# Four gathered value rows per burst, at the highest priority, with seven gather tiles and six steps between U and V

## The chip, the core and the metric

The kernel runs on one core of a Trainium2 chip. A core has five engines with queues of their own, each worked through in order: TensorE (PE; its weight loads are shown as PEld), VectorE (DVE), ScalarE (ACT), GpSimd (POOL) and SyncE (SP). Here SP issues the plain transfers and POOL the gathers. The metric is the device time of one execution in microseconds (us). Before the change it is 3000.16 us, the median of three runs (2996.83 to 3005.19).

## The reference, cut to what matters

Two layers, each a token mixer and then an expert mixer; 512 tokens of width 1024:

```
x = x + sliding_window_attention(rmsnorm(x), ...)      # layer 0
x = x + peer_ffn(rmsnorm(x), ..., peer_u[0], peer_v[0])
x = x + short_gated_conv(rmsnorm(x), ...)              # layer 1
x = x + peer_ffn(rmsnorm(x), ..., peer_u[1], peer_v[1])

def peer_ffn(...):   # per token: 8 heads, 16 of 16384 experts each
    s = scores of the query against 2 x 128 sub keys;  idx, g = top 16 of the sums, softmax
    a = einsum('td,thkd->thk', x, U[idx])
    w = g * gelu(a)
    y = einsum('thk,thkd->td', w, V[idx])
```

So every token needs 128 rows of U and 128 rows of V, of 4 KB each, chosen by its own routing.

## The kernel before, in words

The 512 tokens are four tiles of 128 (0 to 3). The expert mixer treats them in two ways.

**Tiles 2 and 3: dense.** `dense` runs through all 16384 experts in 128 steps of 128. `ustep(i)` loads 512 KB of U, splits it in a high and a low part (ACT casts, DVE subtracts: `uh`, `ul`), multiplies (24 matmuls into `psA`) and takes the gelu into `dw`. `vstep(i)` multiplies `dw` by the gates `G` (POOL or DVE, L713), splits it (`wh`, `wl`), loads and splits 512 KB of V (`vh`, `vl`) and adds 12 matmuls to the four accumulators `y` (L731). U steps run `LAG` = 7 ahead. The gates come from `gen` (L734 on): 64 generations a layer, made in four chunks of 16, each with three DVE operations (`igr`, `oj`, `oi`) and 32 small matmuls into `psG`; a V step needs the whole chunk of its 32 steps. The first chunk stands in a prelude between the routing and the first V step.

**Tiles 0 and 1: gathered.** `gather(l, t)` treats one tile of one layer; the four calls run one after the other. First the U rows: 128 gathers of 128 rows (512 KB, POOL, L631), each followed by a multiply and row sum on DVE (L634, `ug`). Then the V rows: 128 gathers (L662), one for each token, and each token's 128 rows are multiplied by its weights on PE, in matmuls with 32 output columns in the array (L672, `acc`). Tokens come in pairs, so that the two halves of two tokens use the four column groups at once: four matmuls a pair. All gather tiles come from the pool `gat` with `GAT` = 6 buffers (in front of layer 1's dense stage two more).

**Who sets the order.** `merge` interleaves three streams (dense and what precedes it; gathers; a routing stream for tiles 0 and 1) by due times; `DSTEP` = 6.8 for a dense step and `rate()`, 2.4 or 2.5 beside a dense stage, for a gather. That gives each instruction its place and so its priority; `tc.high_priority(offset)` raises it by so many places. A scheduler then writes each engine's queue, taking by priority what it holds to be ready. The queue's order is fixed before the kernel runs. The V matmuls have `HPV` = 600 beside a dense stage and `HPF` = 3000 elsewhere, `gen` has 3000, the U rows' operations on DVE 0. A manual dependency lets the first row's matmuls of a pair wait for the second row's gather, so that a pair stands together.

The calls follow each other as U1, V1 (layer 0, tile 0), U2, V2 (layer 0, tile 1), U3, V3 (layer 1, tile 0), U4, V4 (layer 1, tile 1). In the trace U2, V2 and most of U3 lie beside layer 0's dense stage, V3 beside the convolution and routing of layer 1, U4 and V4 beside layer 1's dense stage.

Of the kernel before, what the change touches and what calls it, by code (L numbers as in the profile page):

```python
# [8 lines left out]
F32 = mybir.dt.float32  # L9
# [10 lines left out]
P = 128  # L20
# [9 lines left out]
NK = 128  # L30
# [3 lines left out]
GONE = -3.0e38  # L34
TG = 16
IC = 32
GAT = 6
RB = 4
HB = 2
LB = 2  # L40
DSTEP = 6.8
LAG = 7
SCB = 4
HPG = 3000
HPT = 0
# [15 lines left out]
VB0 = 1.0  # L61
WPU = 1
WPV = 0
HPV = 600
HPF = 3000
GX0 = 0
FS0 = 1.0
FS1 = 1.0
# [14 lines left out]
def trunk(ctx: ExitStack, tc: tile.TileContext, a: dict, out: bass.AP):  # L83
    nc = tc.nc
# [441 lines left out]
    def router(l, tiles, rpool, psum, xnT, res):  # L526
        gain = gain_of(a["norm_ffn"][l:l + 1, :])
        early = l == 0 and tiles == [0]
        groups = []
        rs = {}  # L530
        dt = [t for t in tiles if t >= 2]
        for t in sorted(tiles, reverse=True):
            if t >= 2:
                rs[t] = route_alloc()
                normT(t, gain, xnT[:, :, (t - 2) * P:(t - 1) * P], psum)
            else:
                h = b4.tile([P, D], F32, name="h", tag="b4")
                norm(t, gain, h)
                nc.sync.dma_start(xnd[t], h)
                hT = gp.tile([P, KC, P], F32, name="hTr", tag="hTr", bufs=1)  # L540
                to_hT(h, hT, psum)
                groups.append((hT, P, [t]))
                if t == 0:
                    rs[t] = route_alloc()
            yield 5.0
        if dt:
            nc.scalar.copy(xh, xnT)
            nc.vector.tensor_tensor(xl, xnT, xh, op=ALU.subtract)
            groups.insert(0, (xnT, 2 * P, dt))
        for h in range(PH):  # L550
            kk = s2.tile([P, 2, NK], F32, name="kk")
            nc.sync.dma_start(kk, a["keysT"][l][:, 2 * h:2 * h + 2, :])
            ws = [piece(a["wq"][l, 2 * h + p]) for p in range(2)]
            for hT, T, js in groups:
                qT = (s2 if T == P else rpool).tile([P, 2, T], F32, name=f"rqT{T}", bufs=2)
                for p in range(2):
                    ps = psum("psrq")
                    if R3[l] and T > P:
                        tg, nb = (("sc", "sc"), SCB) if l == 0 else (("wh", "wl"), WSB)
                        mm3(ps[:, :T], split(ws[p], rpool, tg, nb), (xh, xl), slice(0, T))  # L560
                    else:
                        for k in range(KC):
                            nc.tensor.matmul(ps[:, :T], ws[p][:, k, :], hT[:, k, :],
                                             start=(k == 0), stop=(k == KC - 1))
                    nc.scalar.copy(qT[:, p, :T], ps[:, :T])
                for jj, t in enumerate(js):
                    ps = psum("psrs")
                    for p in range(2):
                        nc.tensor.matmul(ps[:, p * P:(p + 1) * P], qT[:, p, jj * P:(jj + 1) * P],
                                         kk[:, p, :], start=True, stop=True)  # L570
                    sc = s2.tile([P, 2, NK], F32, name="rsc", bufs=3)
                    nc.scalar.copy(sc, ps[:, :2 * P].rearrange("p (m k) -> p m k", m=2))
                    if t == 1:
                        nc.sync.dma_start(scd[h], sc)
                    else:
                        route_head(rs[t], h, sc)
                    if early:
                        decode(rs[t], h, h + 1)
                        expert_idx(rs[t], h, h + 1)
                        if h == 0:  # L580
                            res.append(rs[t])
                        st[f"h0_0_{h}"] = 1
                    elif t >= 2 and h % DEC == DEC - 1:
                        decode(rs[t], h + 1 - DEC, h + 1)
                    yield 4.5 * (3.0 if l == 1 and tiles == [0] else 1.0)
        for t in sorted(rs):
            if t < 2 and not early:
                decode(rs[t], 0, PH)
                expert_idx(rs[t], 0, PH)
            route_end(rs[t], t, psum)  # L590
            if not early:
                res.append(rs[t])
            yield 5.0

    def late_router(l, psum, res):
        r = route_alloc()
        for h in range(PH):
            sc = s2.tile([P, 2, NK], F32, name="rsc", bufs=3)
            nc.sync.dma_start(sc, scd[h])
            route_head(r, h, sc)  # L600
            decode(r, h, h + 1)
            expert_idx(r, h, h + 1)
            if h == 0:
                res.append(r)
            st[f"h{l}_1_{h}"] = 1
            yield LP
        route_end(r, 1, psum)
# [12 lines left out]
    def gather(l, t, r):  # L620
# [5 lines left out]
        for s in range(P):  # L626
            if early and s % TK == 0:
                yield f"h{l}_{t}_{s // TK}"
            h, c = divmod(s, TK)
# [19 lines left out]
        for gr in range(2):  # L649
            acc = pv.tile([P, 512], F32, name="acc", tag="acc")  # L650
            for q in range(4):
                wd = gp.tile([P, 2, 8, 32], F32, name="wd", tag="wd", bufs=2)
                wdf = wd.rearrange("p j r c -> p j (r c)")
                nc.gpsimd.memset(wd, 0.0)
                nc.vector.tensor_copy(wdf[:, :, 8 * q:8 * q + 7 * 33 + 1:33],
                                      wT.rearrange("p (j r) -> p j r", j=4)[:, 2 * gr:2 * gr + 2, 8 * q:8 * q + 8])
                for r8 in range(8):
                    vgs = []
                    for j in range(2):
                        tt = 64 * gr + 32 * j + 8 * q + r8  # L660
                        vg = gtile("vg")
                        ld = nc.gpsimd.indirect_dma_start(  # L662
                            out=vg, out_offset=None, in_=a[f"v{l}"],
                            in_offset=bass.IndirectOffsetOnAxis(ap=idxT[:, tt:tt + 1], axis=0))
                        vgs.append(vg)
                        if j == 0:
                            yield rate()
                    with tc.high_priority(offset=HPF if st.get("front") else HPV):
                        for j in range(2):
                            for h in range(2):  # L670
                                c = 32 * (2 * j + h)
                                mm = nc.tensor.matmul(acc[c:c + 32, :], wd[:, j, r8, :],  # L672
                                                      vgs[j][:, h * 512:(h + 1) * 512],
                                                      start=(q == 0 and r8 == 0), stop=(q == 3 and r8 == 7))
                                if j == 0:
                                    tc.add_manual_dep(mm.ins, ld.ins.name, together, reason="both rows of a pair")
                    yield rate()
            for j in range(2):
                for h in range(2):
# [308 lines left out]
```

## Time and profile before

| | |
|---|---|
| median of three runs | 3000.16 us |
| the profiled execution | 2992.02 us, span 2990.3 us |
| PE, PEld busy | 88%, 70% of the span |
| DVE busy | 75% |
| ACT, POOL busy | 52%, 46% |
| mean transfer rate | 311 GB/s |
| largest single groups | L631 U gathers on POOL 668.3 us, L634 on DVE 622.8 us, L672 V matmuls on PE 318.1 us |

The busy shares are averages over stages with different limits. The page's second part shows it: in some of the 40 slices PE stands at 9, in others DVE. So the span is to be read by stage, and in each stage the engine is to be found that has no idle time.

### The profile page before, as it was taken

The page shows a single profiled execution, that of the slowest core. Times are in us where ns is not written, and L with a number is a line of the kernel's source. Part 1 is how long each engine was busy: PE and PEld are TensorE (multiplying, and loading weights), DVE is VectorE, ACT ScalarE, POOL GpSimd, SP SyncE. Part 2 cuts the span into 40 slices and gives each one's busy share as a digit, 9 for nine tenths or more (in the row PEclk, how much of TensorE's full clock was granted, in tenths as well). Part 3 has the DMA queues.
Part 4 walks back from the last instruction along what each step waited for, and adds up shares of the span by engine and source line. Part 5 has one row for each costly group of instructions (what it writes and reads, how often), then busy time and mean ns, then how long its engine had stood idle before and what let it go on. Part 6 is the DMA issues. An engine that isn't in the chain of part 4 may idle for free. (4 is left out here: it accounts for less than half of the span.)

```text
span 2990.3 us, 53463 instructions
## 1 busy us (share of the span) xinstructions
PE 2626.9 (88%) x19980; PEld 2083.9 (70%) x19980; DVE 2235.7 (75%) x5234; ACT 1559.1 (52%) x2384; POOL 1365.3 (46%) x1154
## 2 busy tenths in 40 slices
PE   5974699869999889999998689997888699999998
PEld 5762368636988767777787686773677577777897
DVE  2499849888998987446699774899899957446554
ACT  4224533685673458348444333358466449547543
POOL 0157733366344455534467424236566755554000
PEclk8986799989999999999999799997999899999999
DMA  5888988989999988998999867789999998998554
GB/s 199 283 315 306 341 293 276 329 308 382 365 353 389 323 318 290 345 328 291 363 408 396 310 220 279 249 319 318 363 349 360 345 359 297 333 317 302 192 189 157
DMA packets 263204, 931.38 MB, mean 311 GB/s; under 512 B 29984, under 2 KB 38560, under 8 KB 262944
## 3 DMA queue, kind: packets, MB, share of 16 engines
q0 software_dynamic: 147456, 536.94, 49.5%
q1 hardware_dynamic: 115488, 391.03, 36.3%
q8 instruction: 157, 2.57, 0.3%
q14 instruction: 103, 0.84, 0.1%
HBM read 916.31 MB, written 11.53 MB: 310 GB/s over the span
## 5 line engine op out<-in xcount | busy, mean ns | idle before, releaser
L631 POOL DMA_INDIRECT ug<-in_u_dram,idx x512 | 668.3, 1305 | 638.1 <-DVE act L634 312.5
L662 POOL DMA_INDIRECT vg<-in_v_dram,idxT x512 | 572.2, 1118 | 689.1 <-PE acc L672 571.7
L634 DVE CUSTOM_DVE_ANT_0 ug<-ug,xn 128x1024 f32<-128x1024 f32 x512 | 622.8, 1226 | 40.3 <-DMA ug<-in_u_dram,idx 39.3
L176 PE MATMUL psA<-xh,uh 128*128 128x256 f32 x2048 | 521.1, 292 | 46.0 <-ACT uh L696 19.0
L177 PE MATMUL psA<-xl,uh 128*128 128x256 f32 x2048 | 504.2, 284 | 0.0
L176 PEld LDWEIGHTS psA<-xh,uh 128*128 128x128 f32 x2048 | 391.1, 191 | 127.9 <-ACT wh L719 32.7
L697 DVE TENSOR_TENSOR ul<-du,uh 128x1024 fp32r<-128x1024 f32 x256 | 316.6, 1237 | 181.0 <-ACT uh L696 179.1
L697 DVE TENSOR_TENSOR vl<-dv,vh 128x1024 fp32r<-128x1024 f32 x256 | 316.2, 1235 | 145.2 <-ACT vh L696 121.8
L177 PEld LDWEIGHTS psA<-xl,uh 128*128 128x128 f32 x2048 | 392.0, 191 | 4.5 <-issue 0.5
L696 ACT CAST uh<-du 128x1024 fp32r<-128x1024 f32 x256 | 268.6, 1049 | 205.3 <-PE psA L177 172.6
L696 ACT CAST vh<-dv 128x1024 fp32r<-128x1024 f32 x256 | 268.5, 1050 | 162.7 <-PE y L731 139.7
L672 PE MATMUL acc<-vg,wd 128*32 128x512 f32 x2048 | 318.1, 635 | 31.4 <-DMA vg<-in_v_dram,idxT 30.9
L731 PE MATMUL y<-vh,wh 128*128 128x512 f32 x1024 | 290.2, 406 | 34.9 <-ACT vh L696 29.9
L179 PE MATMUL psA<-xh,ul 128*128 128x256 f32 x2048 | 288.7, 283 | 10.1 <-DVE ul L697 10.0
L731 PE MATMUL y<-vl,wh 128*128 128x512 f32 x1024 | 285.7, 401 | 12.8 <-DVE vl L697 12.8
L731 PE MATMUL y<-vh,wl 128*128 128x512 f32 x1024 | 285.5, 399 | 3.0 <-DVE wl L720 3.0
L179 PEld LDWEIGHTS psA<-xh,ul 128*128 128x128 f32 x2048 | 261.8, 189 | 21.8 <-DVE ul L697 16.6
L738 ACT COPY jr<-ijg 128x2048 f16<-128x2048 f16 x128 | 243.2, 1900 | 35.0 <-DVE oj L742 33.1
L731 PEld LDWEIGHTS y<-vh,wh 128*128 128x128 f32 x1024 | 179.4, 191 | 86.5 <-ACT vh L696 36.7
L731 PEld LDWEIGHTS y<-vl,wh 128*128 128x128 f32 x1024 | 190.1, 191 | 62.9 <-DVE vl L697 18.8
L731 PEld LDWEIGHTS y<-vh,wl 128*128 128x128 f32 x1024 | 194.8, 192 | 50.9 <-DVE wl L720 4.7
L742 DVE TENSOR_TENSOR oj<-jr,io 128x2048 f16<-128x2048 f16 x128 | 157.4, 1229 | 78.0 <-PE psG L751 66.7
(208 smaller groups left out, 4021.1 us busy)
## 6 DMA issues: line engine op xcount, KB each, us to landing
du<-in_uT_dram SPq DMA_DIRECT2D x256, 512.0 KB, 6.6
dv<-in_v_dram SPq DMA_DIRECT2D x256, 512.0 KB, 5.9
wpc<-in_wq_dram SPq DMA_DIRECT2D x64, 512.0 KB, 4.8
wpc<-in_w_in_dram SPq DMA_DIRECT2D x48, 512.0 KB, 5.9
wpo<-in_wo_dram SPq DMA_DIRECT2D x16, 512.0 KB, 7.5
ug<-in_u_dram,idx POOLq DMA_INDIRECT x512
vg<-in_v_dram,idxT POOLq DMA_INDIRECT x512
wpo<-in_w_out_dram SPq DMA_DIRECT2D x16, 512.0 KB, 5.2
```

The costliest lines, as they stand in the source:

```text
L176: nc.tensor.matmul(ps, w[0][:, k, :], x[0][:, k, ts], start=(k == 0), stop=False)
L177: nc.tensor.matmul(ps, w[0][:, k, :], x[1][:, k, ts], start=False, stop=False)
L179: nc.tensor.matmul(ps, w[1][:, k, :], x[0][:, k, ts], start=False, stop=(k == KC - 1))
L631: nc.gpsimd.indirect_dma_start(out=ug, out_offset=None, in_=a[f"u{l}"], in_offset=bass.IndirectOffsetOnAxis(ap=r["idx"][h][:, c:c + 1], ax ...
L634: nc.vector.tensor_tensor_reduce(out=ug, in0=ug, in1=xn, scale=1.0, scalar=0.0, op0=ALU.mult, op1=ALU.add, accum_out=act[:, s:s + 1])
L662: ld = nc.gpsimd.indirect_dma_start(out=vg, out_offset=None, in_=a[f"v{l}"], in_offset=bass.IndirectOffsetOnAxis(ap=idxT[:, tt:tt + 1], ax ...
L672: mm = nc.tensor.matmul(acc[c:c + 32, :], wd[:, j, r8, :], vgs[j][:, h * 512:(h + 1) * 512], start=(q == 0 and r8 == 0), stop=(q == 3 and ...
L696: nc.scalar.copy(hi, w)
L697: nc.vector.tensor_tensor(lo, w, hi, op=ALU.subtract)
L731: nc.tensor.matmul(ys[tt][h], x[:, tt * P:(tt + 1) * P], m[:, h * 512:(h + 1) * 512], start=first and k == 0, stop=last and k == len(terms ...
L738: nc.scalar.copy(jr, ijg[:, 0, t0:t0 + TG].unsqueeze(2).to_broadcast([P, TG, P]))
L742: nc.vector.tensor_tensor(oj, jr, io128.unsqueeze(1).to_broadcast([P, TG, P]), op=ALU.is_equal)
```

## The change

- A group of V rows is four tokens instead of two (eight matmuls instead of four), and each row's matmuls wait for all later gathers of the group.
- `HPV` and `HPF` become 5000.
- `GAT` is 7, `LAG` is 6 (with two `dw` buffers beyond it, as before), and the score tile `rsc` has two buffers instead of three.

```diff
--- before.py
+++ after.py
@@ -34,12 +34,12 @@
 GONE = -3.0e38
 TG = 16
 IC = 32
-GAT = 6
+GAT = 7
 RB = 4
+LB = 2
 HB = 2
-LB = 2
 DSTEP = 6.8
-LAG = 7
+LAG = 6
 SCB = 4
 HPG = 3000
 HPT = 0
@@ -61,8 +61,8 @@
 VB0 = 1.0
 WPU = 1
 WPV = 0
-HPV = 600
-HPF = 3000
+HPV = 5000
+HPF = 5000
 GX0 = 0
 FS0 = 1.0
 FS1 = 1.0
@@ -568,7 +568,7 @@
                     for p in range(2):
                         nc.tensor.matmul(ps[:, p * P:(p + 1) * P], qT[:, p, jj * P:(jj + 1) * P],
                                          kk[:, p, :], start=True, stop=True)
-                    sc = s2.tile([P, 2, NK], F32, name="rsc", bufs=3)
+                    sc = s2.tile([P, 2, NK], F32, name="rsc", bufs=2)
                     nc.scalar.copy(sc, ps[:, :2 * P].rearrange("p (m k) -> p m k", m=2))
                     if t == 1:
                         nc.sync.dma_start(scd[h], sc)
@@ -595,7 +595,7 @@
     def late_router(l, psum, res):
         r = route_alloc()
         for h in range(PH):
-            sc = s2.tile([P, 2, NK], F32, name="rsc", bufs=3)
+            sc = s2.tile([P, 2, NK], F32, name="rsc", bufs=2)
             nc.sync.dma_start(sc, scd[h])
             route_head(r, h, sc)
             decode(r, h, h + 1)
@@ -654,26 +654,28 @@
                 nc.gpsimd.memset(wd, 0.0)
                 nc.vector.tensor_copy(wdf[:, :, 8 * q:8 * q + 7 * 33 + 1:33],
                                       wT.rearrange("p (j r) -> p j r", j=4)[:, 2 * gr:2 * gr + 2, 8 * q:8 * q + 8])
-                for r8 in range(8):
-                    vgs = []
-                    for j in range(2):
-                        tt = 64 * gr + 32 * j + 8 * q + r8
+                for r8 in range(0, 8, 2):
+                    vgs, lds = [], []
+                    for n in range(4):
+                        tt = 64 * gr + 32 * (n % 2) + 8 * q + r8 + n // 2
                         vg = gtile("vg")
                         ld = nc.gpsimd.indirect_dma_start(
                             out=vg, out_offset=None, in_=a[f"v{l}"],
                             in_offset=bass.IndirectOffsetOnAxis(ap=idxT[:, tt:tt + 1], axis=0))
                         vgs.append(vg)
-                        if j == 0:
+                        lds.append(ld)
+                        if n < 3:
                             yield rate()
                     with tc.high_priority(offset=HPF if st.get("front") else HPV):
-                        for j in range(2):
+                        for n in range(4):
+                            j, r = n % 2, r8 + n // 2
                             for h in range(2):
                                 c = 32 * (2 * j + h)
-                                mm = nc.tensor.matmul(acc[c:c + 32, :], wd[:, j, r8, :],
-                                                      vgs[j][:, h * 512:(h + 1) * 512],
-                                                      start=(q == 0 and r8 == 0), stop=(q == 3 and r8 == 7))
-                                if j == 0:
-                                    tc.add_manual_dep(mm.ins, ld.ins.name, together, reason="both rows of a pair")
+                                mm = nc.tensor.matmul(acc[c:c + 32, :], wd[:, j, r, :],
+                                                      vgs[n][:, h * 512:(h + 1) * 512],
+                                                      start=(q == 0 and r == 0), stop=(q == 3 and r == 7))
+                                for ld in lds[n + 1:]:
+                                    tc.add_manual_dep(mm.ins, ld.ins.name, together, reason="rows of four")
                     yield rate()
             for j in range(2):
                 for h in range(2):
```

Counted in the order of both kernels (PE and DVE; a U row is one L634 multiply, a burst is a run of V matmuls with nothing else between):

| stretch | before | now |
|---|---|---|
| V1 pairs ahead of the first U step of dense 0 | 30 | 38 |
| prelude of dense 0: U rows | 0 | 6 |
| U2 in dense 0 | 128 rows, 49 steps, 16 generations | 122 rows, 36 steps, 17 |
| V2 | 64 pairs in 54 bursts, 47 steps, 31 generations | 64 in 33, 47.7 steps, 18 |
| U3 in dense 0 | 83 rows, 32 steps, 0 generations | 102 rows, 29 steps, 13 |
| dense 0 after these rows | 0 steps | 15 steps |
| layer 1 ahead of its first U step: U3 rows, V3 pairs | 45, 30 | 26, 42 |
| prelude of dense 1: U rows | 0 | 28 |
| U4 in dense 1 | 128 rows, 42 steps, 16 generations | 100 rows, 29 steps, 12 |
| V4 | 64 pairs in 56 bursts, 50 steps, 31 generations | 64 in 32, 45 steps, 21 |
| dense 1 after V4 | 36 steps, 0 generations | 54 steps, 15 |
| bursts in all | 222 | 129 |

Three places. First PE in V2, where the V matmuls (`acc`) stand between the parts of dense steps (`psA` of a U step, `y` of a V step). Before:

```order
L731 MATMUL y_4417<-vl,wh 128x512
L731 MATMUL y_4418<-vl,wh 128x512
L731 MATMUL y_4419<-vl,wh 128x512
L731 MATMUL y_4420<-vl,wh 128x512
L672 MATMUL acc<-vg,wd 32x512 x4
L176 MATMUL psA<-xh,uh 128x256
L177 MATMUL psA<-xl,uh 128x256
```

and now:

```order
L176 MATMUL psA<-xh,uh 128x256
L177 MATMUL psA<-xl,uh 128x256
L179 MATMUL psA<-xh,ul 128x256 x2
L674 MATMUL acc<-vg,wd 32x512 x8
L179 MATMUL psA<-xh,ul 128x256 x6
L733 MATMUL y_4417<-vh,wh 128x512
L733 MATMUL y_4418<-vh,wh 128x512
```

A burst holds eight matmuls instead of four, and stands inside the run of a U step rather than between two steps.

Second, DVE at the end of layer 1's prelude, up to the first `wl` of its dense stage. `igr`, `oj` and `oi` are a generation, `G<-G` and `dw` the products with the gates, `ab` belongs to tile 1's routing. Before:

```order
L745 TENSOR_TENSOR igr<-igr,io_107 128x512
L493 CAST idx<-idxf 128x16
L473 SCALAR_TENSOR_TENSOR ab<-ab 128x16
L747 TENSOR_TENSOR oi<-igr 128x1024
L713 TENSOR_TENSOR G<-G 128x256 x8
L713 TENSOR_TENSOR dw<-dw,G 128x256 x7
L474 TENSOR_TENSOR ab<-sel,ab 128x16
L742 TENSOR_TENSOR oj<-jr,io_107 128x2048
L745 TENSOR_TENSOR igr<-igr,io_107 128x512
L720 TENSOR_TENSOR wl<-G,wh 128x256 x2
```

and now:

```order
L744 TENSOR_TENSOR oj<-jr,io_107 128x2048
L747 TENSOR_TENSOR igr<-igr,io_107 128x512
L634 ISA ug,act<-ug,xn 128x1024
L634 ISA act 128x1
L715 TENSOR_TENSOR G<-G 128x256 x8
L715 TENSOR_TENSOR dw<-dw,G 128x256 x4
L749 TENSOR_TENSOR oi<-igr 128x1024
L715 TENSOR_TENSOR dw<-dw,G 128x256 x2
L722 TENSOR_TENSOR wl<-G,wh 128x256 x2
```

U rows (L634) of tile 1 now stand among the prelude's generations; there are 28 of them ahead of the first `wl`, and there were none.

Third, DVE near the 112th V step of layer 0's dense stage, before:

```order
L697 TENSOR_TENSOR vl<-dv,vh 128x1024
L634 ISA ug,act<-ug,xn 128x1024
L634 ISA act 128x1
L713 TENSOR_TENSOR dw<-dw,G 128x256
L697 TENSOR_TENSOR ul<-du,uh 128x1024
L634 ISA ug,act<-ug,xn 128x1024
L634 ISA act 128x1
L720 TENSOR_TENSOR wl<-dw,wh 128x256
```

and now:

```order
L699 TENSOR_TENSOR vl<-dv,vh 128x1024
L715 TENSOR_TENSOR dw<-dw,G 128x256
L699 TENSOR_TENSOR ul<-du,uh 128x1024
L722 TENSOR_TENSOR wl<-dw,wh 128x256
L715 TENSOR_TENSOR dw<-dw,G 128x256
L699 TENSOR_TENSOR vl<-dv,vh 128x1024
L699 TENSOR_TENSOR ul<-du,uh 128x1024
L722 TENSOR_TENSOR wl<-dw,wh 128x256
```

The U rows of tile 0 for layer 1, which stood between the splits to the end of the stage, have come earlier; the last 15 steps have none.

## Rows read from the trace of the kernel before

**Rows 1.** Windows, all engines: window and its length, busy us (instructions), PE clock, DMA share

```profile
core 0: us, PE busy (x) PEld busy (x) DVE busy (x) ACT busy (x) POOL busy (x), PEclk, DMA share, GB/s
0.00:537.00 537.00, 402.84 (x2618) 307.68 (x2618) 378.96 (x1392) 202.35 (x517) 220.19 (x202) 0.87 0.82 287
...
672.00:1083.00 411.00, 373.28 (x2809) 322.92 (x2810) 378.56 (x796) 216.84 (x322) 192.10 (x161) 0.98 0.96 359
1083.00:1462.00 379.00, 377.77 (x3235) 280.69 (x3233) 213.54 (x266) 239.01 (x319) 177.15 (x160) 1.00 0.88 316
1462.00:1645.00 183.00, 163.65 (x992) 141.90 (x984) 181.87 (x280) 76.88 (x116) 124.38 (x89) 1.00 1.02 400
1645.00:1965.00 320.00, 278.75 (x1743) 230.18 (x1743) 227.53 (x719) 107.09 (x190) 115.92 (x105) 0.94 0.75 261
1965.00:2092.00 127.00, 101.33 (x1146) 66.66 (x1145) 118.95 (x474) 103.91 (x121) 69.91 (x64) 0.87 0.94 337
2092.00:2403.00 311.00, 253.92 (x1834) 209.84 (x1835) 298.12 (x464) 173.15 (x222) 207.80 (x146) 0.92 0.96 356
2403.00:2797.00 394.00, 393.58 (x3349) 295.27 (x3348) 219.06 (x263) 247.32 (x332) 187.69 (x172) 1.00 0.87 310
```

**Rows 2.** Waits of the whole span: us in total, times, longest us

```profile
POOL vg L662 <- PE acc L672: 571.7, 169, 33.4
...
ACT rsc L572 <- PE psrs L569: 79.2, 41, 4.0
...
PE acc L672 <- DMA vg<-in_v_dram,idxT: 30.9, 28, 4.3
...
PE psT L375 <- DVE h L146: 24.2, 3, 17.2
```

**Rows 3.** Chain of waits inside dense 1: start us, length us, engine and line

```profile
2544.34 0.81 PE psG L751 x32
...
2550.38 5.69 DMA vg<-in_v_dram,idxT
...
2590.63 2.73 PE y L731 x12
...
2597.39 2.72 PE y L731 x12
...
2651.47 2.72 PE y L731 x12
...
2659.07 2.72 PE y L731 x12
...
2805.12 2.77 PE y L731 x12
...
2810.72 2.77 PE y L731 x12
```

**Rows 4.** Timeline of DVE in U4: start us, length us

```profile
2266.55 1.21 DVE L634 CUSTOM_DVE_ANT_0 ug<-ug,xn 128x1024 f32<-128x1024 f32 x1
...
2267.69 1.22 DVE L697 TENSOR_TENSOR ul<-du,uh 128x1024 fp32r<-128x1024 f32 x1
...
2269.97 0.42 DVE L745 TENSOR_TENSOR igr<-igr,io 128x512 f16<-128x512 f16 x1
2270.31 1.27 DVE L742 TENSOR_TENSOR oj<-jr,io 128x2048 f16<-128x2048 f16 x1
2271.50 1.21 DVE L634 CUSTOM_DVE_ANT_0 ug<-ug,xn 128x1024 f32<-128x1024 f32 x1
...
2272.65 1.22 DVE L697 TENSOR_TENSOR vl<-dv,vh 128x1024 fp32r<-128x1024 f32 x1
2273.78 0.41 DVE L720 TENSOR_TENSOR wl<-dw,wh 128x256 fp32r<-128x256 f32 x1
2274.12 1.22 DVE L634 CUSTOM_DVE_ANT_0 ug<-ug,xn 128x1024 f32<-128x1024 f32 x1
...
2276.40 0.68 DVE L747 TENSOR_TENSOR oi<-igr 128x1024 f16<-128x1024 f16 x1
2277.00 1.22 DVE L634 CUSTOM_DVE_ANT_0 ug<-ug,xn 128x1024 f32<-128x1024 f32 x1
```

## The prediction

> **What bounds the kernel now.** I read the windows first, cut where the gather stream goes from U to V rows and where a dense stage begins or ends [rows 1]. The reader is to see an alternation. Where V rows are beside dense steps, PE has no idle time: 377.8 of 379 us in V2, 393.6 of 394 us in V4. Where U rows are, DVE is the full one: 378.6 of 411 us in U2, 181.9 of 183 us in U3, 298.1 of 311 us in U4; PE idles there for 38, 19 and 57 us. In the prelude of layer 1 (1965 to 2092) DVE has 119.0 of 127 us and PE 101.3. So a unit of work costs what the engine that is full in its stretch takes for it, and nothing on the other. Next I read prices from the chain of waits for PE [rows 3] and from DVE's timeline in a full stretch [rows 4].
>
> PE: a dense step alone takes 2810.72 - 2805.12 = 5.60 us, with one pair 2597.39 - 2590.63 = 6.76, with two pairs in one burst 2659.07 - 2651.47 = 7.60 [rows 3]. The first pair of a burst costs 1.16 us, the second 0.84, so each burst that is saved gives 0.32 us. A generation takes 0.81 us of PE [rows 3]; I take 1.2 with the gap around it, because V2 then comes out: 47 x 5.60 + 31 x 1.2 + 64 x 0.84 + 54 x 0.32 = 371 us against 379.
>
> DVE, by the starts of what follows [rows 4]: a U row 2267.69 - 2266.55 = 1.14 us; a split 2273.78 - 2272.65 = 1.13; `wl` 0.34; `igr` 0.34, `oj` 1.19, `oi` 0.60. The product with the gates is of the size of `wl` and is on DVE about every other step, 0.17. So a dense step costs DVE 2 x 1.13 + 0.34 + 0.17 = 2.77 us, a generation 2.13. U3 checks it: 83 x 1.14 + 32 x 2.77 = 183 us, as the window has. U4: 128 x 1.14 + 42 x 2.77 + 16 x 2.13 = 296 against 311.
>
> **The change part by part.** The groups of four do what they say: 129 bursts for 222. 45 of the 93 that go were in V2 and V4, where PE is full: 45 x 0.32 = 14 us. But the new order also shifts the gather stream against the dense steps, and that decides more. V1 and V3 end sooner, U rows come sooner and closer together (3.4 a step in U2 instead of 2.6), and fewer dense steps are done beside them. U rows are the work that fills DVE; a step moved out of their stretch saves 2.77 us there and costs 5.60 us where PE is alone.
>
> Layer 0's dense stage, from the counts. U2: 6 rows, 13 steps fewer, one generation more: -6.8 - 36.0 + 2.1 = -41 us; its 32 us of DVE idle stay or go as the rows close up, so -41 to -73, and I take the middle, -57. V2: 13 generations and 21 bursts fewer, 0.7 steps more: -15.6 - 6.7 + 3.9 = -18. U3: 102 x 1.14 + 29 x 2.77 + 13 x 2.13 = 224 us and then 15 steps without rows, 84 us: 308 against 183, +125. Sum +50, with ends at +34 and +66.
>
> Layer 1's dense stage. U4: 28 rows, 13 steps and 4 generations fewer: -31.9 - 36.0 - 8.5 = -76. V4 and what follows: 13 steps and 5 generations more, 24 bursts fewer: +72.8 + 6.0 - 7.7 = +71. Sum -5. The 28 rows have gone into the prelude ahead of the first V step: 28 x 1.14 = 32 us on a DVE that has 8 idle. They cost between nothing, if the routing work of tile 1 makes room by going earlier, and 32; I take 16.
>
> Layer 1 ahead of its U steps (1645 to 1965): 19 U3 rows fewer, -22 us of DVE, of which DVE is busy 228 of 320; PE waits there 24.2 us for the normed tiles on DVE [rows 2], so the gain is between 0 and 22; I take -11. 12 V pairs more, 12 x 0.84 = 10 us, beside 41 us of PE idle: 0 to +10, I take 0. Layer 0 ahead of its U steps: 8 pairs more, 0 to +7 us, with PE busy 403 of 537: 0.
>
> `LAG` 6: one U step, 2.8 us of PE, goes from each prelude into the stage, and U2 and U4 have PE idle to hide it; without that 5.6 us. `rsc` with two buffers: ACT's copy into it waits 79.2 us in all for its matmuls [rows 2], which will come no sooner, so I take nothing; if the buffer came last instead, the cost would be at most what PE then loses in the routing, and I hold up to 10 us for it.
>
> The wait that is added: the last row of a group gets its tile from the first row of the group before (seven tiles: four and three), so its gather starts only after that burst. Behind a waiting matmul stands all of PE. From the gather's start to its landing the chain shows 5.69 us [rows 3], with up to 2 us on POOL ahead of it. In V2 and V4 the order puts 8 to 10 us of other PE work between two bursts, so it fits narrowly. Now PE waits for V rows 30.9 us in 28 places [rows 2], 1.1 us each. Ends: 0 us, and 64 groups at 1.1, 70 us; I take 0, since POOL mostly waits for PE (571.7 us [rows 2]) and not the other way.
>
> Sum: 50 - 5 + 16 - 11 = +50 us. On the profiled execution's 2992 us that is 3042. That execution lies 8 us below the median of the runs, 3000; on the median it is 3050.
>
> The Trainium skill, Perfetto Trace Analysis, section Optimization Strategy, says of kernels whose most-contended engine changes over time that interleaving the regimes may help. The windows agree: U3 before is the best mixed stretch, DVE 181.9 and PE 163.7 of 183 us [rows 1]; by that rule a coarser mix loses, which is the direction of my sum.
>
> **The rivals.** *Bursts decide* (faster). The scheduler may have put U rows early where DVE would idle on the chip too, so that nothing of the shift reaches PE, and the fewer bursts stay: 93 x 0.32 = -30 us, 2970. For it: V stretches have PE full, and the V matmuls there cost 64 x 1.16 = 74 us each. Against it: DVE has only 1 to 32 us idle in U2, U3 and U4 [rows 1], too little for the rows. It decides if the 15 last steps of dense 0 are gained back in U2. The Trainium skill, TensorEngine Tiling (Array Packing), section Key Properties, states that a change of the tiling mode drains TensorE; by it all of the price would lie in the number of bursts. The 0.32 us a burst agrees, and it is too little for that.
>
> *It cancels* (no change). Layer 0's dense stage at its low end, +34, the prelude's rows hidden, the 22 us in front of it gained whole, and the 14 us of bursts already in it: 34 - 5 - 22 = +7, 3007.
>
> *The fourth row is late* (slower still). If landings are some 2 us longer than the one shown, every group in V2 and V4 waits, and the pairs no longer hide it. 64 x 1.1 = +70 on part of the sum, say 50 + 45: 3095. For it: one group and three rows in flight instead of three pairs. Against it: the 8 to 10 us between bursts.
>
> That the change doesn't do what it says is excluded by the order.
>
> **How the numbers follow.** My forecast 0.53, the late fourth row 0.10, the bursts 0.23, cancelling 0.14. What a measurement can tell is about 0.3%, 9 us: so 0.62 slower, 0.25 faster and 0.13 the same, with the edges of the cases shared out. The sum of the low ends is 34 - 5 - 22 = +7, of the high ends 66 - 5 + 32 + 10 + 7 + 6 + 10 = +126; the likeliest case's own range is 3007 to 3095. With the bursts' case taken in below, 2968 to 3095.
>
> **What would show it.** In the new profile: a stretch of some 15 steps at the end of layer 0's dense stage with PE full and DVE half idle, and U2 and U3 with DVE full and more PE idle than 38 and 19 us; U2 shorter than 411 by 40 to 70 us; layer 1's prelude longer than 127 us with U rows in it; U4 near 235 us instead of 311. V bursts of two pairs with steps of 7.6 us. PE's wait for V rows below 60 us; above 100 the late fourth row is right. I am wrong if PE's idle time falls in the U stretches, or if layer 0's dense stage, first V step to last, keeps its 973 us or is shorter.

## The result, and the profile after

The changed kernel takes 3040 us (median; 3032 to 3055) against 3000 for the kernel before on the same chip: ratio 1.0146, 95% interval 1.0121 to 1.017. It is slower, and 10 us below the forecast of 3050. The profiled execution has a span of 3035.6 us against 2990.3, so 45.3 us more; the forecast's sum was +50 on that execution.

The windows of the new profile, cut at the same events as [rows 1], are these (columns as there); in order: U2, V2, U3 with the steps after it, the last 83 us of that stretch by themselves, the front of layer 1, its prelude, U4, V4, and the end of dense 1.

```profile
669.00:1021.00 352.00, 309.19 (x2393) 269.74 (x2394) 331.10 (x731) 182.16 (x268) 162.82 (x131) 0.95 0.96 365
1021.00:1375.00 354.00, 348.16 (x2789) 269.83 (x2791) 195.33 (x241) 200.36 (x273) 181.50 (x170) 1.00 0.92 330
1375.00:1683.00 308.00, 259.68 (x1866) 224.82 (x1859) 262.97 (x398) 152.85 (x213) 162.15 (x109) 0.94 0.85 317
1600.00:1683.00 83.00, 81.59 (x489) 72.49 (x488) 44.24 (x55) 38.59 (x57) 2.88 (x2) 1.00 0.50 165
1683.00:2006.00 323.00, 277.70 (x1845) 231.99 (x1843) 211.85 (x706) 110.78 (x196) 117.33 (x114) 0.94 0.76 269
2006.00:2163.00 157.00, 89.79 (x1030) 64.82 (x1030) 144.21 (x490) 103.35 (x116) 94.35 (x76) 0.75 0.89 315
2163.00:2386.00 223.00, 174.30 (x1242) 144.58 (x1246) 217.68 (x361) 112.69 (x150) 147.12 (x102) 0.92 0.95 358
2386.00:2728.00 342.00, 339.34 (x2831) 262.43 (x2823) 192.54 (x224) 209.05 (x277) 186.47 (x166) 1.00 0.92 331
2728.00:3024.00 296.00, 295.62 (x2257) 265.54 (x2253) 178.76 (x230) 180.44 (x257) 11.93 (x8) 1.00 0.51 171
```

The reader is to see two things. First, the fourth row: PE has 81.6 of 83 us, DVE 44.2, so DVE stands idle for 39 us beside the last steps of dense 0. Those are steps that U rows used to stand beside. Second, the U stretches (U2, the part of U3 ahead of 1600, U4) are full on DVE and leave PE 43, 47 and 49 us idle. The part of U3:

```profile
1375.00:1600.00 225.00, 178.09 (x1380) 152.34 (x1373) 218.73 (x343) 114.26 (x156) 159.27 (x107) 0.92 0.98 372
```

The DMA engines are nearly full in these stretches too (share 0.96, 0.98 and 0.95), so the landing of the U rows could set the pace as well as DVE. It does not: DVE's waits for it, in the three stretches in turn, are small.

```profile
DVE ug L634 <- DMA ug<-in_u_dram,idx: 4.9, 4, 2.5
DVE ug L634 <- DMA ug<-in_u_dram,idx: 0.2, 1, 0.2
DVE ug L634 <- DMA ug<-in_u_dram,idx: 1.4, 2, 1.1
```

The granted clock is lower than before in two of them, 0.95 in U2 (0.98) and 0.92 in that part of U3 (1.00). But DVE is idle for only 21, 6 and 5 us in the three stretches, and no more than that can have gone to a slower PE in them. The whole of dense 0 in one window, before and then after:

```profile
672.00:1645.00 973.00, 914.70 (x7027) 745.52 (x7027) 773.98 (x1340) 532.73 (x756) 493.62 (x409) 0.99 0.94 350
```

```profile
669.00:1683.00 1014.00, 917.04 (x7041) 764.40 (x7042) 789.40 (x1368) 535.38 (x753) 506.47 (x410) 0.96 0.91 338
```

PE is busy for about as long, 915 and 917 us; what grew by 39 us is PE's idle time, 58 to 97. By stage, from the first and last `y` and `psA` matmuls of each dense stage in the two traces, before and after: up to the first V step 672.3 and 669.0 us; dense 0 971.9 and 1014.2; the front of layer 1 321.1 and 322.7; its prelude 126.6 and 157.5; dense 1 886.0 and 859.8; what follows 12.4 and 12.4. The differences are -3, +42, +2, +31 and -26.

Of the prelude's 157 us the last 47 are these:

```profile
2116.00:2163.00 47.00, 4.12 (x128) 3.80 (x128) 44.07 (x85) 21.88 (x21) 38.31 (x31) 0.50 0.91 326
```

DVE is busy for 44 us there, most of them with 26 of the 28 U rows, and PE for 4. So the rows came last in the prelude, where PE has next to no work beside them. The prelude's clock, 0.75 on the mean, is at its lower level (0.50 of 2.4 GHz) through all of these 47 us.

The waits that answer to [rows 2], and one burst in V4 (PE's timeline: start us, length us):

```profile
POOL vg L662 <- PE acc L674: 469.9, 119, 60.4
...
ACT rsc L572 <- PE psrs L569: 33.9, 21, 3.7
...
PE acc L674 <- DMA vg<-in_v_dram,idxT: 34.8, 19, 5.5
...
PE psT L375 <- DVE h L146: 20.6, 2, 14.2
```

```profile
2445.92 1.07 PE L733 MATMUL y<-vh,wh 128*128 128x512 f32 x4
...
2450.99 1.92 PE L674 MATMUL acc<-vg,wd 128*32 128x512 f32 x16
...
2453.53 1.09 PE L733 MATMUL y<-vh,wh 128*128 128x512 f32 x4
```

PE's wait for V rows is 34.8 us in 19 places, against 30.9 in 28, although the gathers took 7.0 us at the median from issue to landing (part 6 of the profile's page) and the forecast had counted 5.69. ACT's wait for the router's matmuls is 33.9 us, where it was 79.2. A step with a burst is 2453.53 - 2445.92 = 7.61 us, what a step with two pairs in one burst took before [rows 3].

### The profile page after: what moved, and what is told of

Same layout as the page of the kernel before. It is cut to its first block, busy times and chain, and to the rows that moved or that the text cites. A ratio compares the mean times of both kernels' runs of the same rounds, so it can differ in the third digit from the quotient of the medians.

```text
span 3035.6 us, 53514 instructions
## 1 busy us (share of the span) xinstructions
PE 2587.7 (85%) x19980; PEld 2107.1 (69%) x19980; DVE 2235.2 (74%) x5233; ACT 1558.4 (51%) x2382; POOL 1374.9 (45%) x1155
## 5 line engine op out<-in xcount | busy, mean ns | idle before, releaser
L662 POOL DMA_INDIRECT vg<-in_v_dram,idxT x512 | 561.8, 1097 | 603.2 <-PE acc L674 469.9
L634 DVE CUSTOM_DVE_ANT_0 ug<-ug,xn 128x1024 f32<-128x1024 f32 x512 | 616.5, 1218 | 43.8 <-DMA ug<-in_u_dram,idx 43.2
L179 PE MATMUL psA<-xh,ul 128*128 128x256 f32 x2048 | 295.6, 286 | 15.9 <-DVE ul L699 15.9
L674 PE MATMUL acc<-vg,wd 128*32 128x512 f32 x2048 | 264.3, 634 | 35.0 <-DMA vg<-in_v_dram,idxT 34.8
L733 PEld LDWEIGHTS y<-vh,wh 128*128 128x128 f32 x1024 | 183.2, 195 | 96.0 <-ACT vh L698 45.3
L715 POOL TENSOR_TENSOR dw<-dw,G 128x256 f32<-128x256 f32 x95 | 121.3, 1278 | 208.8 <-ACT dw L709 160.3
```

Source lines behind the costliest of these rows:

```text
L179: nc.tensor.matmul(ps, w[1][:, k, :], x[0][:, k, ts], start=False, stop=(k == KC - 1))
L634: nc.vector.tensor_tensor_reduce(out=ug, in0=ug, in1=xn, scale=1.0, scalar=0.0, op0=ALU.mult, op1=ALU.add, accum_out=act[:, s:s + 1])
L662: ld = nc.gpsimd.indirect_dma_start(out=vg, out_offset=None, in_=a[f"v{l}"], in_offset=bass.IndirectOffsetOnAxis(ap=idxT[:, tt:tt + 1], ax ...
L674: mm = nc.tensor.matmul(acc[c:c + 32, :], wd[:, j, r, :], vgs[n][:, h * 512:(h + 1) * 512], start=(q == 0 and r == 0), stop=(q == 3 and r ...
L715: (nc.gpsimd if (WPU if st.get("gu") else WPV) else nc.vector).tensor_tensor(w, w, G[:, i % GR, :], op=ALU.mult)
L733: nc.tensor.matmul(ys[tt][h], x[:, tt * P:(tt + 1) * P], m[:, h * 512:(h + 1) * 512], start=first and k == 0, stop=last and k == len(terms ...
```

## The experiments

Ratios are to the kernel before on the same chip, with 95% intervals. The kernel before ran at 3000 us beside hold_u3, hold_u4, six_tiles and pairs, at 2998 beside rows_back, spread_fours, spread_pairs and lag_only, and at 3050 on the chip of the last four, which are therefore compared by ratio; a ratio times 3000 stands beside it where microseconds help.

**Holding the U rows.** Five experiments change nothing in the source of the changed kernel but where U rows may stand (hold_u3, hold_u4, rows_back, spread_fours, spread_thin); spread_pairs and spread_old do the same to two other kernels. A row's multiplication on DVE is made to follow the `wl` of a given V step, also on DVE, so no wait between engines is added. The `yield` holds the row's gather, and all gathers behind it, back in `merge` until that step has been written, and the scheduler then writes a new order around the rows. `HOLD` gives for a (layer, tile) the dense layer, the first step and the rows per step:

```diff
+HOLD = {(1, 0): (0, 96, 2.6)}
...
+        d, n0, per = HOLD.get((l, t), (0, NK, 1.0))
         for s in range(P):
+            n = n0 + int(s / per)
+            if n < NK:
+                yield f"w{d}_{n}"
...
-                nc.vector.tensor_tensor_reduce(out=ug, in0=ug, in1=xn, ...
+                row = nc.vector.tensor_tensor_reduce(out=ug, in0=ug, in1=xn, ...
+            if n < NK:
+                tc.add_manual_dep(row.ins, st[f"w{d}_{n}"], together, reason="row after step")
...
-                nc.vector.tensor_tensor(wl, w, wh, op=ALU.subtract)
+                split = nc.vector.tensor_tensor(wl, w, wh, op=ALU.subtract)
+                st[f"w{l}_{i}"] = split.ins.name
```

**hold_u3** is the changed kernel with that.

> The changed kernel, but the U rows of tile 0 for layer 1 (U3) may not be multiplied before the split of w of V step 96 + s/2.6 of layer 0's dense stage (s is the row's number). Nothing else is touched: groups of four, seven tiles, priorities and lag stay. By the order U3 then stands in steps 97 to 127 instead of 85 to 110, 63 rows are left for layer 1 instead of 26, and 4 rows of U4 stand in layer 1's prelude instead of 28. Theory (the place of the U rows costs the time): dense 0 loses the 15 to 18 steps at its end that have PE alone; priced as in the forecast it goes from 1014 us to about 935; the 37 rows more ahead of layer 1's U steps cost 0 to 42 us, I take 20; the prelude falls from 157 by 24 to 30; dense 1 grows by about 20. Sum -66: about 2975 us, 2950 to 3010. Rival (the time goes in waits for the rows of a group, or in the tiles, the lag or the router's buffer): these are as in the changed kernel, so it stays at 3030 to 3050.

Measured: 2994 us (2987 to 2999), ratio 0.9977 (0.9963 to 0.999). 47 us come back although groups, tiles, priorities and lag are those of the changed kernel; the rival, 3030 to 3050, is out. The windows of U3, of the front of layer 1 and of its prelude:

```profile
1464.00:1642.00 178.00, 168.28 (x1034) 148.15 (x1033) 165.55 (x248) 78.53 (x117) 101.45 (x67) 1.00 0.96 352
1642.00:1964.00 322.00, 273.86 (x1796) 234.32 (x1797) 252.11 (x791) 111.75 (x198) 161.26 (x139) 0.92 0.87 316
1964.00:2105.00 141.00, 103.20 (x1110) 67.30 (x1109) 118.06 (x443) 102.62 (x116) 76.82 (x63) 0.85 0.85 299
```

Dense 0 is back at 970 us. That is 44 of the 80 that the prices gave: the mixed stretch at its end has DVE at 166 and PE at 168 of 178 us, so neither is quite full. The front takes 322 us with 40 us more of DVE work in it than in the changed kernel (252.1 against 211.9), so no cost of the rows there can be seen; I had taken 20.

**hold_u4** has `HOLD = {(1, 1): (1, 4, 3.4)}` instead.

> The changed kernel, but the U rows of tile 1 for layer 1 (U4) may not be multiplied before the split of w of V step 4 + s/3.4 of layer 1's dense stage. Everything ahead of layer 1's prelude stays as it is. By the order no U row stands in the prelude (28 before), and U4 stands in steps 5 to 42 instead of up to 29. Theory (28 rows in the prelude cost there what DVE takes for them): the prelude falls from 157 to about 127 us, U4 grows from 223 by about 73, the rest of dense 1 shrinks by about 50: sum about -8, 3032 us, 3015 to 3045. Rival (the prelude is bound by its generations and the routing, and the rows are hidden in it): the prelude stays at 150 to 157, dense 1 grows by 22, sum +22, 3060 us. Second rival (the prelude's low granted clock, 0.75, makes it long): it falls below 120 with a higher clock.

Measured: 3035 us (3022 to 3040), ratio 1.0113 (1.0079 to 1.0147), which by itself can't be told from the changed kernel. The windows can. The prelude, now without U rows:

```profile
2008.00:2144.00 136.00, 91.61 (x1063) 66.57 (x1062) 118.42 (x454) 106.17 (x119) 60.20 (x50) 0.79 0.77 273
```

It is 136 us instead of 157, with PE's work nearly the same (91.6 and 89.8) and DVE's 26 us less; dense 1 is 878 instead of 860, +18. So the 28 rows cost 21 us in the prelude and give 18 back in dense 1. The clock went only from 0.75 to 0.79, and the prelude did not fall below 120 us, so the second rival is out.

**six_tiles**

```diff
-GAT = 7
+GAT = 6
```

> The changed kernel with six gather tiles instead of seven. Groups of four stay (130 bursts), but now two rows of each group get their tiles from the burst before, not one. By the order the U rows go back to about where they stood before the change: U2 in steps 6 to 50, U3 in 95 to 127 with 39 rows left, 3 rows of U4 in the prelude. Theory (the place of the U rows): dense 0 about -60, the 13 rows more ahead of layer 1's U steps 0 to 15, the prelude -25, dense 1 +16: about 2975 us, so faster than the kernel before the change too. Rival (late rows): with two rows late in each group PE waits in both V stretches, 64 groups by 1.1 us or more on top of that: 3045 us or slower, and PE's wait for V rows rises from 35 us to 100 or more.

Measured: 3049 us, ratio 1.0167 (1.0139 to 1.0194). The rival is right here. The rows went back, and dense 0 with them (974 us), but PE waits:

```profile
PE acc L674 <- DMA vg<-in_v_dram,idxT: 107.0, 52, 5.2
```

72 us more of it than in the changed kernel, and 3049 lies 74 above what I expected without it. So two late rows in a group show at about the price of the rival, 64 groups by 1.1 us; the one late row of seven tiles hardly does.

**pairs** is the kernel before with all of the change but the groups of four (`GAT = 7`, `LAG = 6`, `HPV = HPF = 5000`, `rsc` with two buffers).

> The kernel before the change with everything of the change but the groups of four: seven tiles, the highest priority, lag six, two router buffers, and pairs. By the order 245 bursts instead of 129, and the U rows early as in the changed kernel (U2 in 0 to 37, U3 in 78 to 104 with 26 rows left, 31 rows of U4 in the prelude). Theory (tiles, priority and lag bring the U rows forward, and that costs; a burst saved gives 0.32 us where PE is full): dense 0 +6, dense 1 +8, prelude +3 against the changed kernel: about 3057 us, 3040 to 3075. Rival (the groups of four cost the time, by the wait for a fourth row): at 3000 us or below, as the kernel before.

Measured: 3044 us (3043 to 3046), ratio 1.0154 (1.0134 to 1.0174), below the 3057 I took and in its range. So the loss is there without any group of four, and on top of it the groups change nothing that can be told (1.0146 with them). Its end of dense 0 looks like the changed kernel's:

```profile
1600.00:1691.00 91.00, 91.00 (x549) 80.96 (x547) 48.63 (x62) 41.70 (x62) 2.60 (x2) 1.00 0.50 165
```

**rows_back** is the changed kernel, complete, with `HOLD = {(0, 1): (0, 5, 2.9), (1, 0): (0, 94, 3.2), (1, 1): (1, 4, 3.4)}`.

> The changed kernel with all of its parts (groups of four, seven tiles, highest priority, lag six, two router buffers), but with the U rows held to about the steps where they stood before the change: U2 in 6 to 49 of dense 0 (before 5 to 49), U3 in 95 to 126 with 46 rows left (before 97 to 127, 45 left), U4 in 5 to 43 of dense 1 (before 5 to 42), none in the prelude. So it shows what the parts of the change are worth by themselves. Theory (the place of the U rows is all of the loss, and the saved bursts give 0.32 us each where PE is full): dense 0 about 958 us against 972, dense 1 about 876 against 886, the prelude 127 to 136: about 2973 us, 2955 to 2995, faster than before. Rival (the lag, the priority or the wait for a group's rows cost by themselves): 3000 us or more although the rows are back.

Measured: 2988 us (2978 to 2999), ratio 0.9957 (0.9943 to 0.9972). With the rows where they were, the change is 13 us faster than the kernel before (0.43% of 3000), and by the medians 52 us faster than without holding. This is the plainest answer: the order with the U rows early costs more than the whole loss. The gain left over is half of what the bursts should have given by 2973.

**spread_fours** has `HOLD = {(0, 1): (0, 3, 2.5), (1, 0): (0, 86, 2.5), (1, 1): (1, 3, 2.5)}` on the changed kernel.

> The changed kernel with the U rows held to 2.5 a step, the pace at which a V step (5.60 us on PE, 2.77 on DVE) and the rows beside it (1.14 each on DVE) fill both engines: U2 in 4 to 54, U3 in 100 to 127 with 45 left, U4 in 4 to 54 of dense 1. Theory (a stretch costs what its full engine takes, and an even mix costs least): dense 0 about 965 us, dense 1 about 855, the prelude about 136: 2961 us, 2940 to 2985. Rival (in a mixed stretch both engines wait for each other through the copies on ScalarE, so a thinner mix only lengthens the stretch): no better than with the rows held at the old pace, 2990 us or more.

Measured: 2945 us (2943 to 2952), ratio 0.9828 (0.9801 to 0.9854): faster than both kernels. Dense 0 and dense 1 in one window each:

```profile
676.00:1628.00 952.00, 897.45 (x7009) 750.67 (x7010) 770.81 (x1328) 526.11 (x749) 495.62 (x395) 0.99 0.94 349
2078.00:2928.00 850.00, 803.32 (x6289) 668.28 (x6290) 624.50 (x861) 501.31 (x682) 384.06 (x302) 0.98 0.84 302
```

PE's idle time in dense 0 falls from 97 to 55 us, and its busy time by 20 as well, at a mean granted clock of 0.99 against 0.96.

**spread_pairs** has the same `HOLD` on the kernel called pairs.

> As the kernel with pairs and all else of the change, with the U rows held to 2.5 a step (U2 in 5 to 54, U3 in 95 to 127 with 46 left, U4 in 4 to 54 of dense 1); 242 bursts. Against the same placing with groups of four it shows what the bursts are worth. Theory (0.32 us for each burst where PE is full, V2 and V4): about 60 bursts more there, +10 to +20 us against the groups of four: about 2975 us. Rival (the wait for a group's fourth row takes that back): the same as or faster than the groups of four.

Measured: 2963 us, ratio 0.9884 (0.9857 to 0.9911), 17 us above the groups of four, inside the 10 to 20 expected; every execution of it (2956 to 2967) is above every one with fours (2943 to 2952). With the rows in place the groups of four are worth about what 0.32 us a burst makes of them, 60 x 0.32 = 19 us.

**lag_only** is the kernel before with

```diff
-LAG = 7
+LAG = 6
...
-                    sc = s2.tile([P, 2, NK], F32, name="rsc", bufs=3)
+                    sc = s2.tile([P, 2, NK], F32, name="rsc", bufs=2)
```

> The kernel before the change with lag six and two router buffers and nothing else. By the order the U rows stay about where they were (U2 in 7 to 50, U3 in 99 to 127 with 48 left, U4 in 5 to 41 of dense 1, none in the prelude). Theory (the forecast's: both are hidden): 2995 to 3008 us, the same as before within what can be told. Rival (the U step that leaves each prelude, 2.8 us each, or the router's buffer costs): +6 to +16 us, up to 3016.

Measured: 3036 us, ratio 1.0112 (1.0078 to 1.0146). Theory and rival both missed: by the ratio +34 us, with the U rows where they were. In the traces dense 0 is 35 us longer (1007 against 972) and dense 1 10. Some 19 of the 35 are in U2 with the steps just ahead of it, 430 us instead of 411, with PE busy for 393 instead of 373; why is open. The other half is in U3:

```profile
1480.00:1681.00 201.00, 164.00 (x970) 141.07 (x968) 182.71 (x275) 75.14 (x113) 145.12 (x88) 0.99 0.96 359
```

DVE's 182.7 and PE's 164.0 us are what they were before, 181.9 and 163.7, but in 201 us instead of 183 [rows 1]. Neither engine is full. PE's waits in that stretch name the third engine, ACT, first in lag_only, then in the kernel before:

```profile
PE y L731 <- ACT vh L696: 19.9, 14, 1.5
PE psA L176 <- ACT uh L696: 15.8, 11, 1.4
```

```profile
PE psA L176 <- ACT uh L696: 15.8, 11, 1.4
PE y L731 <- ACT vh L696: 2.9, 2, 1.5
```

17 us more of waiting for the copy `vh`. One of the 14 places, in the timeline of lag_only (in brackets the idle time ahead and who ended it):

```profile
1565.74 1.10 PE L179 MATMUL psA<-xh,ul 128*128 128x256 f32 x8
...
1566.88 0.38 ACT L707 ACTIVATE dw<-psA 128x256 f32<-128x256 f32 x1 [2.43 <-PE psA L179]
...
1567.16 1.04 ACT L696 CAST vh<-dv 128x1024 fp32r<-128x1024 f32 x1
...
1568.25 1.19 PE L731 MATMUL y<-vh,wh 128*128 128x512 f32 x4 [1.41 <-ACT vh L696]
```

On ACT `vh` stands behind `dw`, which has to wait for the U step's last matmul, and PE's next matmul needs `vh`. So each such step has ACT's two copies in a row on the path. Whether another order on ACT alone would give the 17 us back was not tried on the chip.

**lag_rsc3** is the kernel before with `LAG = 6` alone.

> The kernel before the change with lag six alone; the router keeps its three buffers. It parts the two edits that together took the kernel before from 2998 to 3036 us. If the lag costs that (the dense stages were longer, the router's place was not): 3025 to 3045 us. If the router's two buffers cost it: 2993 to 3005 us.

Measured: ratio 1.0052 (1.0031 to 1.0072), 16 us of 3000. It falls between the two answers: the lag has about half of the loss, and the other half came only with the router's two buffers. In its trace U3 is as long as before (183 us), and PE waits for `vh` as little as before:

```profile
1498.00:1682.00 184.00, 160.96 (x976) 139.72 (x972) 179.86 (x276) 75.28 (x113) 125.01 (x87) 1.00 1.01 391
...
PE y L731 <- ACT vh L696: 2.9, 2, 1.5
```

On ACT `vh` stands directly behind `dw` in 2 places of this stretch, as in the kernel before, and in 13 of lag_only's U3. So the lag of six does not by itself bring the order that cost lag_only's U3 18 us. That order came with the router's two buffers, although no copy of the router stands in that stretch. This points to the order that the scheduler makes of the edits together, rather than to a price of either. Where the 16 us of lag_rsc3 are can't be told, as no profile of the kernel before was taken on that chip.

**priority_only** is the kernel before with `HPV = HPF = 5000` alone.

> The kernel before the change with the highest priority for the V matmuls and nothing else: lag seven, six tiles, pairs, three router buffers. By the order U2 stands in steps 2 to 45, U3 in 89 to 121 with 30 rows left, 26 rows of U4 in layer 1's prelude. Theory (the place of the rows): dense 0 about +14 us, the prelude about +20, dense 1 about -25: 3005 us, 2990 to 3020. Rival (the lag was the costly part in pairs and the priority adds nothing, or gives the V rows their time back): 2985 to 2998. Second rival (matmuls at the highest priority stand in PE's queue ahead of work that is ready, and PE waits for V rows): 3020 us or more, PE's wait for V rows over 60 us.

Measured: ratio 0.9943 (0.9923 to 0.9964), 17 us faster; the theory is wrong by some 20 us and the first rival right in its direction, even beyond its range (2983 by ratio). PE's wait for V rows is 9.1 us in its trace, so the second rival is out. The highest priority by itself is no part of the loss, although it too brings U rows forward: U3 ends 33 us ahead of the end of dense 0, and 26 rows stand in the prelude of layer 1. So a shift of that size did not cost on the whole what the prices said.

**spread_thin** is the changed kernel with `HOLD = {(0, 1): (0, 3, 2.3), (1, 0): (0, 98, 2.0), (1, 1): (1, 3, 2.3)}`.

> As the changed kernel with its rows held to 2.5 a step, but thinner: U2 2.3 a step (steps 4 to 60), U3 2.0 (steps 104 to 127, 81 rows left for layer 1's front, where DVE had room for them at no cost before), U4 2.3 (steps 4 to 59). Theory (a stretch costs what its full engine takes, and PE is the full one once the rows are thin enough): dense 0 falls from 952 to about 925 us, dense 1 stays near 845, the front of layer 1 rises by 0 to 15: 2925 us, 2905 to 2945. Rival (at 2.5 the mix is already even, and the rows that are pushed out cost as much in the front of layer 1): 2945 us or more.

Measured: ratio 0.9825 (0.9787 to 0.9863), the same as at 2.5 a step (0.9828): 2947 by ratio. The theory's 2925 is outside the interval (2936 to 2959 by ratio) and the rival's 2945 or more fits; no gain from a mix thinner than 2.5 can be seen.

**spread_old** is the kernel before with the `HOLD` of spread_fours.

> The kernel before the change, all of it (pairs, six tiles, lag seven, old priorities, three router buffers), with its U rows held to 2.5 a step: U2 in steps 5 to 54, U3 in 105 to 127 with 69 rows left, U4 in 12 to 54 of dense 1. It asks whether the lag of six costs in any order. Theory (lag six cost 38 us only through the queue order that it happened to bring, so with the rows held anew nothing of it is left): pairs and old priorities 2955 to 2985 us, above the 2945 of the changed kernel with held rows. Rival (lag six costs about 38 us by itself, in any order): about 2925 us, below the changed kernel with held rows.

Measured: ratio 0.9913 (0.9881 to 0.9944), 2974 by ratio, as the theory has it. Lag seven with three buffers gives no 38 us once the rows are held; the changed kernel's parts, held the same way, are 0.85% faster. So the lag's cost is not a price by itself.

## Why the prediction was right, and where its terms were not

**The main term held.** The direction, and the mechanism that most of the sum rests on, were right. Dense 0 was forecast at +50 us and came at +42. Its parts: U2 -57 forecast, -59 measured; V2 -18 and -25; U3 with the steps after it +125 and +125 (308 us, as worked out). The 15 steps with PE full and DVE half idle are there. That the place of the rows is the cause, and not only beside it, is shown by hold_u3 (-47 us), rows_back (-52 us) and spread_fours (-95 us), which keep every part of the change. One reservation stays: each hold also gives the other engines a new order, and lag_only shows that such an order can cost 34 us with the rows in place. That four held orders with different places of the rows (spread_thin is the fourth) all gain 47 us or more speaks against chance.

**Dense 1** was forecast at -5 and came at -26: U4 is 88 us shorter (76 forecast), V4 with the end 63 longer (71 forecast). **The prelude** was forecast at +16, the middle between 0 and 32, and came at +31: the routing work of tile 1 made no room, and 26 of the rows came last, beside 4 us of PE. hold_u4 parts that: the 28 rows cost 21 us, and 10 us are there without them. What those are stays open; with the rows of all three calls held the prelude has about 128 us again (rows_back and spread_fours), so the change's parts do not cost them by themselves. That the two errors, -21 and +15, nearly cancel is luck.

**The front of layer 1** was forecast at -11 for 19 U3 rows fewer and came at +2. The step that failed is that DVE's load there reaches the end of the stretch: hold_u3 puts 40 us more of DVE work there and takes the same 322 us. The upper end, 0, was right.

**Lag and router buffer at nothing.** This step was wrong where it could be measured: on the kernel before the two cost 34 us, twice the 6 and 10 that I held. The cover I named (PE idle in U2 and U4) did not hide them; in U3, where 18 us of it are, the loss goes with the order on ACT. In the changed kernel's windows no such term shows: the sum of dense 0 comes out without it. That these two terms could be left out of the sum was luck, as nothing in the forecast said that the edits would not add up: 34 for lag and buffers and -17 for the priority on the kernel before make 17, but all three with seven tiles make 46 (pairs). Which part of the remaining 29 belongs to the seven tiles was not tried alone.

**The late fourth row** at nothing: right, 34.8 us of waiting against 30.9. six_tiles shows that the reserve is one tile. Its size, 107 us for two late rows in a group, is nearer to my upper end of 70 than to nothing.

**The bursts.** 14 us were taken for the groups of four in V2 and V4. At the same places of the rows they give 17 (spread_fours against spread_pairs); in the changed kernel, against pairs, only 3, which can't be told from nothing; the rows stand elsewhere in each of the two. The rival by which the bursts decide failed at its own condition: U2 did not gain back the last 15 steps, PE's idle time in U2 and U3 grew from 38 and 19 us to 43 and 47. In U4 it fell from 57 to 49 us, in a stretch 88 us shorter; my sign of being wrong did not provide for that.

**The range.** My high ends add up to +126 us, 3126; its top of 3095 came from the late fourth row instead. The measured time is near neither.

**The rule** that a stretch costs what its full engine takes priced the coarse stretches to a few us. It can fail where two engines are near full together: hold_u3's dense 0 (44 us gained of 80) and lag_only's U3 (201 us with 183 of work). By the rule of the Trainium skill that I had cited (Perfetto Trace Analysis, section Optimization Strategy), interleaving the regimes may help. spread_fours agrees, 43 us below rows_back, which has the same parts with the rows at their old, coarser places; spread_thin shows where it stops.

## What to carry to other kernels

Count the work beside each step, not only the work an edit removes: a stream with more buffers or a higher priority can run ahead, bunch up on the second engine and leave the first alone later. If that is seen in the order, hold the stream to the pace at which both engines fill (here 2.5 rows a step) by a dependency inside one engine; no cost of it was seen, and it turned a 1.5% loss into a 1.7% gain. And measure an edit's parts together as well as alone: through a scheduler their costs did not add.

## What was not expected of the hardware

The same kernel before took 2998 to 3000 us on two chips and 3050 (3037 to 3060, 17 runs) on a third; no profile of it on that one was taken, so where the 50 us are is open. Two engines that are near full together can lose a tenth when the order on a third changes: DVE's 182 and PE's 164 us of U3 fitted in 183 us before and took 201 in lag_only. And a low mean clock need not be a cause: PE's granted clock in the prelude of layer 1 was 0.75 on the mean, against 0.87 before, but it was at the half level (1.2 GHz) for all of the last 47 us, in which PE had 4 us of work and DVE set the pace.
